# Moving one pooling product behind the first selected queries, and raising the priority of the compression inputs

## Chip, cores and metric

One NeuronCore of a Trainium2 chip. The metric is the device time of one execution in microseconds (us).

## The reference

One decoder layer on x of 512 tokens by 1024 channels. One input projection of x feeds three token mixers: A, a pooling mixer (trailing windows of 2, 4, 8 and 16 tokens, one for each of four channel groups); B, attention over the top 128 keys that an indexer picks for each query; C, attention over compressed blocks, selected blocks and a window, with gates. Each output is multiplied by a SiLU gate, projected, merged by sigmoid gates, projected again, added to x and normalised. The two parts that the change touches:

```
# A, for channel group g with window w
mean   = (running sum over the last w tokens) / min(position, w)
pooled = mean - x_g
y_g    = (pooled @ pool_w[g] + pool_b[g]) * scale_g          # then * silu(a_z)

# C, compressed keys and values: 31 blocks of 32 tokens, stride 16
blk = tok[block] + pos            # per group: 31 x (32 * 64)
h   = silu(blk @ w1)
out = h @ w2                      # kcmp from c_kc, vcmp from c_vc
```

## The kernel before, in words

Float32 products are made of three matmuls (`mm3`, lines 68 to 70): both operands are split into a high and a low part (`split`, lines 64 and 65: ScalarE writes the high part, VectorE subtracts for the low one). A dense tile (`dense`) is 128 output channels by 512 tokens, eight such triples over the 1024 input channels; its weight tile is loaded and split by `load_w` (lines 92 to 95: a DMA issued by POOL, ScalarE's copy, POOL's subtraction), two to three tiles ahead.

The order of TensorE's instructions is the order in which the program emits them. VectorE, ScalarE, POOL and SyncE are ordered by a scheduler that simulates the program on its own model and takes, among the instructions that are ready, the one with the highest priority; earlier in the program is higher, and `tc.high_priority()` raises what stands inside it. Buffers carry a tag, and tiles of one tag share a fixed number of buffers ("s" 2, "b" 6, "t" 16, dense PSUM 3, score PSUM 4): a tile can be written only when an earlier one is free.

Attention runs through a list of units. For each sub-unit `front` emits score matmuls (`qkc`, line 441), whose mask is VectorE's (443), exponent ScalarE's (448), and whose probabilities are split by both (460 and 462); `back` two sub-units later emits the products with the values (479). Between them a stream F of other work is advanced by a count of steps (`F.step`), one step for each yield. F's items are written out by hand: compression, gates, pooling, queries, merges. A string such as "c0" in the list is a marker: F stops there until the flag is set, which happens when the last unit of group 0 of mixer C is finished.

What the change touches in F:
- `compress_in(i, nm)`, for keys and then for values: loads `w1` into `w1s` (tag s) and splits it into `w1h` and `w1l`; runs a dense tile; adds bias and position in four VectorE instructions into `bk` (tag s, line 331); splits `bk` into `bkh` and `bkl`. `compress_mid` multiplies them later (names `cpk`, `cpv`).
- `pool_x(g)`: a dense tile, ScalarE's copy `x0`, g + 1 doubling sums on POOL (lines 566 and 567), VectorE's mean minus x (570 to 573), a split into `ph`. `pool_z(g)`: the gate `za`. `pool_y(g)`: one triple `ph` times the pooling weights, then VectorE (588) and a split into `YA`, which the `merge` items read.
- `f_zc(1, 1)`: the second gate tile of group 1 of mixer C. `f_qb(0, e)`: the queries of mixer B, the first work behind "c0".

In profile lines, `d` is a dense tile's PSUM, `pool` the PSUM of `pool_y`, `is` and `rel` the indexer's scores, `acc` of lines 294 to 306 the indexer's sum and its top-k.

Of the kernel before, what the change touches and what calls it, by code (L numbers as in the profile page):

```python
# [12 lines left out]
OP = mybir.AluOpType  # L13
# [21 lines left out]
def trunk(ctx, tc, a, out, dbg=None):  # L35
    nc = tc.nc
# [11 lines left out]
    def big(tag, name, dt=F32, shape=(128, 2, 512)):  # L48
        return bp.tile(list(shape), dt, tag=tag, name=name, bufs=BUFS[tag])
# [4 lines left out]
    def dps(name):  # L54
        return pd.tile([128, 512], F32, tag="pd", name=name)

    def qps(name):
        return pq.tile([128, 512], F32, tag="pq", name=name)

    def f(ap):  # L60
        return ap.bitcast(F32)

    def split(h, l, src):
        nc.scalar.activation(h, src, AF.Copy)
        nc.vector.tensor_sub(l, src, f(h))  # L65
# [35 lines left out]
    ps = qps("idle")  # L101
# [40 lines left out]
    def dense(i, s0=0, ps=None):  # L142
        wh, wl = early[i][1:] if i in early else load_w(a["wt"][i], 1024, f"w{i}")
        ps = (ps or dps)(f"d{i}")
        n = S - s0
        for k in range(KT):
            w = slice(k * 128, k * 128 + 128)
            mm3(ps[:, :n], wh[:, w], wl[:, w], X(0, k, s0), X(1, k, s0), k == 0, k == KT - 1)
            yield
        return ps[:, :n], bias[:, i:i + 1]  # L150
# [7 lines left out]
    LOW, UPP = slice(0, 64), slice(64, 128)  # L158
# [160 lines left out]
    def compress_in(i, nm):  # L319
        pos = small["pos" + nm]  # L320
        w1s = big("s", "w1s", F32, (128, 16, 64))
        w1h = big("t", "w1h", F32R, (128, 16, 64))
        w1l = big("t", "w1l", F32R, (128, 16, 64))
        nc.sync.dma_start(w1s, a["w1" + nm])
        split(w1h, w1l, w1s)
        ps, b = yield from dense(i)
        bk = big("s", "bk", F32, (128, 2, 31, 16))
        for g in range(2):
            r = (LOW, UPP)[g]
            for hf in range(2):  # L330
                nc.vector.scalar_tensor_tensor(
                    bk[64 * hf:64 * hf + 64, g],
                    ps[r, 16 * hf:16 * hf + 496].rearrange("p (n l) -> p n l", l=16), b[r],
                    pos[r, None, 16 * hf:16 * hf + 16].to_broadcast([64, 31, 16]),
                    op0=OP.add, op1=OP.add)
        bh = big("t", "bkh", F32R, (128, 62, 16))
        bl = big("t", "bkl", F32R, (128, 62, 16))
        split(bh, bl, bk.rearrange("p g n l -> p (g n) l"))
        CP[nm] = w1h, w1l, bh, bl

    def compress_w2(nm, m):
# [389 lines left out]
    for n in (2, 1, 1, 1, 1, 1, 2):  # L731
        for _ in range(n):
            st.step()
        for _ in range(n):
            st2.step()
    Stream([(index_queries, 0), (f_qc, 0, 0), (values_load,), (index_queries, 1), (f_qc, 0, 1), (values,)]).rest()
    mcmp, rowv = small["mcmp"].rearrange("p (j n) -> p j n", j=NT), small["rowv"]
    POOL[0] = True
    F = Stream([(compress_in, I_KC, "k"), (vscales,), (compress_in, I_VC, "v"), (f_zc, 0, 0), (compress_mid, "k"),
                (f_zc, 0, 1), (compress_k,), (compress_mid, "v"), (f_qc, 1, 0), (f_qc, 1, 1), (compress_v,),  # L740
                (early_g, 0, 0), (f_kk, 1), (early_g, 0, 1), (f_pool,), (f_zc, 1, 0), (pool_x, 0), (early_g, 0, 2),
                (pool_z, 0), (pool_x, 1), (early_g, 0, 3), (pool_y, 0), (pool_z, 1), (f_zc, 1, 1), (pool_x, 2), (pool_y, 1),
                (pool_z, 2), (pool_x, 3), (pool_y, 2), (pool_z, 3), (pool_y, 3),
                "c0", (f_qb, 0, 0), (f_qb, 0, 1)] + [(merge, 0, d) for d in range(3)] + [(f_zb, 0, 0), (f_zb, 0, 1)] +
               [(merge, 0, d) for d in range(3, 7)] + [(early_g, 2, 0), (merge, 0, 7)] +
               [(early_g, 2, d) for d in range(1, 4)] +
               ["c1", (f_qb, 1, 0), (f_qb, 1, 1), (f_zb, 1, 0), (f_zb, 1, 1)] + [(merge, 2, d) for d in range(KT)])
# [54 lines left out]
    for w in work:  # L802
        kind, g, j, br = w
# [91 lines left out]
    for t in range(NT):  # L895
        last = t == NT - 1
        for c0, c1 in ((512, 768), (768, 1024)) if last else ((512, 1024),):
            ps = dps("wo")
# [98 lines left out]
```

## Time and profile before

| | |
|---|---|
| median of 3 runs (lowest to highest) | 541.46 us (541.25 to 541.78) |
| profiled execution | 540.3 us, span 538.5 |
| mean granted TensorE clock | 0.982 |
| PE busy | 517.8 us (96%) |
| VectorE (DVE) busy | 377.3 us (70%) |
| ScalarE (ACT) busy | 278.1 us (52%) |
| POOL busy | 215.9 us (40%) |

The span is the time from the first to the last instruction of the profiled execution. A timeline row gives the start, the duration, the engine, the line of the kernel, the operation with its tiles (out<-in) and shape, how many instructions the row merges, and in brackets the idle time of the engine before it with what ended it. Matmuls are pipelined, so that a start follows the start before by less than the duration shown.

### The profile page before, as it was taken

Reading aid. Unit: us, or ns where it says so; the run is one execution under the profiler, and the core shown is the slowest. Engines: PE = TensorE matmul, PEld = TensorE weight load, DVE = VectorE, ACT = ScalarE, POOL = GpSimd, SP = SyncE. Lnnn points to the kernel's source line nnn. Section 1 sums busy time; section 2 is a strip of 40 time slices with the busy share of each in tenths; the row PEclk is TensorE's granted clock in tenths of the full one; section 3 lists DMA queues with packets and bytes.
Section 4 is the critical chain, followed back from the end, with each engine's and each line's share of the span. In section 5 each row is a group of like instructions: output and inputs, shape, how many; then the busy total and the mean of one; then the engine's idle time right before and its main releaser. Section 6 shows DMA issues by size and latency. Waiting matters only on the chain.

```text
span 538.5 us, 7778 instructions
## 1 busy us (share of the span) xinstructions
PE 517.8 (96%) x2718; PEld 419.3 (78%) x2718; DVE 377.3 (70%) x928; ACT 278.1 (52%) x561; POOL 215.9 (40%) x190
## 2 busy tenths in 40 slices
PE   8999999999999997799999899999999999999993
PEld 4889878888778875577788687877777888887883
DVE  5774898898769888678777887957653444544276
ACT  6783465667555767264644547666663334442000
POOL 0425433436455476126344444426662211215043
PEclk9999989999999999699999999999999999999997
DMA  7622331374464434064544645462654445453012
GB/s 275 264 79 79 103 133 60 83 152 119 147 138 119 121 90 117 23 134 130 144 120 84 146 128 107 121 130 65 181 147 121 121 139 190 158 205 126 1 65 91
DMA packets 82135, 66.72 MB, mean 124 GB/s; under 512 B 67184, under 2 KB 68656, under 8 KB 82096
## 3 DMA queue, kind: packets, MB, share of 16 engines
q1 hardware_dynamic: 74912, 40.54, 29.1%
q0 software_dynamic: 7184, 25.69, 14.9%
q8 instruction: 21, 0.34, 0.3%
q14 instruction: 18, 0.15, 0.1%
HBM read 47.87 MB, written 2.10 MB: 93 GB/s over the span
## 4 chain that ended last, share of the span: by engine, by line
PE 87%; DVE 5%; DMA 3%; ACT 2%; issue 1%; POOL 1%; SPq 0%; DVEq 0%; ACTq 0%; POOLq 0%
PE d L68 18%; PE d L69 17%; PE d L70 17%; PE acc L479 4%; PE pp L68 4%; PE qkc L441 4%; PE pp L69 4%; PE pp L70 4%; PE wo L70 3%; PE wo L69 2%; PE wo L68 2%; PE qkb L441 2%; DMA wo_st<-in_wo_dram 2%; DMA xst<-in_xT_dram 1%; PE acc L529 1%; PE ve L69 1%
## 5 line engine op out<-in xcount | busy, mean ns | idle before, releaser
L68 PE MATMUL d<-xh,w_h 128*128 128x512 f32 (+1 forms) x424 | 168.3, 397 | 0.0
L69 PE MATMUL d<-xl,w_h 128*128 128x512 f32 (+1 forms) x424 | 165.6, 391 | 0.0
L70 PE MATMUL d<-xh,w_l 128*128 128x512 f32 (+1 forms) x424 | 165.5, 390 | 0.0
L95 POOL TENSOR_TENSOR w_l<-w_st,w_h 128x1024 fp32r<-128x1024 f32 x41 | 98.1, 2394 | 128.9 <-ACT w_h L93 124.8
L68 PEld LDWEIGHTS d<-xh,w_h 128*128 128x128 f32 x424 | 80.5, 190 | 17.9 <-issue 3.2
L70 PEld LDWEIGHTS d<-xh,w_l 128*128 128x128 f32 x424 | 80.2, 189 | 17.0
L69 PEld LDWEIGHTS d<-xl,w_h 128*128 128x128 f32 x424 | 80.4, 190 | 13.8
L93 ACT ACTIVATE w_h<-w_st 128x1024 fp32r<-128x1024 f32 x53 | 56.2, 1060 | 37.0 <-DMA w_st<-in_wt_dram 26.8
L448 ACT ACTIVATE qkc<-qkc,nb 128x512 f32<-128x512 f32 (+3 forms) x64 | 32.1, 502 | 51.1 <-DVE nb L443 28.3
L95 POOL TENSOR_TENSOR wp_l<-wp_st,wp_h 128x512 fp32r<-128x512 f32 x16 | 20.6, 1288 | 52.2 <-ACT wp_h L93 52.2
L460 ACT ACTIVATE pc<-qkc,r 128x512 f16<-128x512 f32 (+3 forms) x64 | 29.6, 527 | 19.7 <-DVE r L456 8.7
L462 DVE SCALAR_TENSOR_TENSOR pc<-qkc,r,pc 128x512 f16<-128x512 f32 (+3 forms) x64 | 32.3, 545 | 9.7 <-ACT pc L460 9.2
L640 POOL TENSOR_TENSOR m<-m,tg 128x512 f32<-128x512 f32 x12 | 16.5, 1378 | 53.7 <-DVE tg L614 53.6
L443 DVE CUSTOM_DVE_ANT_0 qkc<-qkc,cmask 128x512 f32<-128x512 f32 (+3 forms) x64 | 31.3, 493 | 3.7 <-PE qkc L441 3.4
L92 POOL DMA_DIRECT2D w_st<-in_wt_dram x41 | 23.3, 569 | 10.2 <-POOL w_l L95 5.9
L70 PE MATMUL wo<-woh,ml 128*128 128x512 f32 (+1 forms) x72 | 26.4, 367 | 0.5 <-DVE ml L65 0.5
L69 PE MATMUL wo<-wol,mh 128*128 128x512 f32 (+1 forms) x72 | 26.3, 366 | 0.0
L68 PE MATMUL wo<-woh,mh 128*128 128x512 f32 (+1 forms) x72 | 26.3, 365 | 0.0
L306 DVE MATCH_REPLACE8 acc<-m,acc 128x256 f32<-128x256 f32 (+2 forms) x48 | 25.8, 541 | 0.0
L305 DVE MAX8 m<-acc 128x8 f32<-128x256 f32 (+2 forms) x48 | 25.4, 549 | 0.0
L68 PE MATMUL pp<-yh,wp_h 128*128 128x512 f32 x64 | 25.3, 395 | 0.0
L69 PE MATMUL pp<-yl,wp_h 128*128 128x512 f32 x64 | 25.0, 390 | 0.0
(249 smaller groups left out, 1003.1 us busy)
## 6 DMA issues: line engine op xcount, KB each, us to landing
w_st<-in_wt_dram POOLq DMA_DIRECT2D x41, 512.0 KB, 3.7
w_st<-in_wt_dram SPq DMA_DIRECT2D x12, 512.0 KB, 4.2
wp_st<-in_wp_dram POOLq DMA_DIRECT2D x16, 256.0 KB, 3.0
wo_st<-in_wo_dram SPq DMA_DIRECT2D x8, 512.0 KB, 3.5
xst<-in_xT_dram SPq DMA_DIRECT2D x8, 256.0 KB, 5.1
wp_st<-in_wp_dram SPq DMA_DIRECT2D x8, 256.0 KB, 2.7
z<-in_x_dram SPq DMA_DIRECT2D x4, 512.0 KB, 5.5
wvst<-in_wve_dram SPq DMA_DIRECT2D x4, 320.0 KB, 7.1
```

The lines of the kernel that those rows point to most:

```text
L68: nc.tensor.matmul(ps, wh, rh, start=start, stop=False)
L69: nc.tensor.matmul(ps, wh, rl, start=False, stop=False)
L70: nc.tensor.matmul(ps, wl, rh, start=False, stop=stop)
L93: nc.scalar.activation(h[:, :n], st, AF.Copy)
L95: eng.tensor_sub(l[:, :n], st, f(h[:, :n]))
L305: nc.vector.max(m8, negm[j])
L306: nc.vector.match_replace(negm[j], m8, negm[j], MARK)
L441: nc.tensor.matmul(ps[:, o:o + m], q, K[:, z, w], start=z == 0, stop=z == 1)
L443: nc.vector.tensor_tensor_reduce(sc[i], sc[i], self.mask, -0.125, 3e38, OP.add, OP.min, nb[:, i:i + 1])
L448: nc.scalar.activation(sc[i], sc[i], AF.Exp, scale=-1.0, bias=nb[:, i:i + 1], accum_out=den[:, i:i + 1])
L460: nc.scalar.activation(p[:, 0, i], sc[i], AF.Copy, scale=r[:, i:i + 1])
L462: self.last = nc.vector.scalar_tensor_tensor(p[:, 1, i], sc[i], r[:, i:i + 1], p[:, 0, i], op0=OP.mult, op1=OP.subtract)
```

## The change

Two edits. In `compress_in` the four VectorE additions and the split of `bk` come inside `tc.high_priority()`; the tiles `bkh` and `bkl` are declared ahead of it. In the list of F, `f_zc(1, 1)` goes from ahead of `pool_x(2)` to behind `pool_x(3)`, `pool_y(2)` from ahead of `pool_z(3)` to behind it, and `pool_y(3)` from ahead of the marker "c0" to between `f_qb(0, 0)` and `f_qb(0, 1)`.

```diff
         ps, b = yield from dense(i)
         bk = big("s", "bk", F32, (128, 2, 31, 16))
-        for g in range(2):
-            r = (LOW, UPP)[g]
-            for hf in range(2):
-                nc.vector.scalar_tensor_tensor(
-                    bk[64 * hf:64 * hf + 64, g],
-                    ps[r, 16 * hf:16 * hf + 496].rearrange("p (n l) -> p n l", l=16), b[r],
-                    pos[r, None, 16 * hf:16 * hf + 16].to_broadcast([64, 31, 16]),
-                    op0=OP.add, op1=OP.add)
         bh = big("t", "bkh", F32R, (128, 62, 16))
         bl = big("t", "bkl", F32R, (128, 62, 16))
-        split(bh, bl, bk.rearrange("p g n l -> p (g n) l"))
+        with tc.high_priority():
+            for g in range(2):
+                r = (LOW, UPP)[g]
+                for hf in range(2):
+                    nc.vector.scalar_tensor_tensor(
+                        bk[64 * hf:64 * hf + 64, g],
+                        ps[r, 16 * hf:16 * hf + 496].rearrange("p (n l) -> p n l", l=16), b[r],
+                        pos[r, None, 16 * hf:16 * hf + 16].to_broadcast([64, 31, 16]),
+                        op0=OP.add, op1=OP.add)
+            split(bh, bl, bk.rearrange("p g n l -> p (g n) l"))
         CP[nm] = w1h, w1l, bh, bl
...
-                (pool_z, 0), (pool_x, 1), (early_g, 0, 3), (pool_y, 0), (pool_z, 1), (f_zc, 1, 1), (pool_x, 2), (pool_y, 1),
-                (pool_z, 2), (pool_x, 3), (pool_y, 2), (pool_z, 3), (pool_y, 3),
-                "c0", (f_qb, 0, 0), (f_qb, 0, 1)] + [(merge, 0, d) for d in range(3)] + [(f_zb, 0, 0), (f_zb, 0, 1)] +
+                (pool_z, 0), (pool_x, 1), (early_g, 0, 3), (pool_y, 0), (pool_z, 1), (pool_x, 2), (pool_y, 1),
+                (pool_z, 2), (pool_x, 3), (f_zc, 1, 1), (pool_z, 3), (pool_y, 2),
+                "c0", (f_qb, 0, 0), (pool_y, 3), (f_qb, 0, 1)] + [(merge, 0, d) for d in range(3)] + [(f_zb, 0, 0), (f_zb, 0, 1)] +
```

## Rows read from the trace of the kernel before

**Rows 1.** The page: busy time, share of the span, instructions.

```profile
PE 517.8 (96%) x2718; PEld 419.3 (78%) x2718; DVE 377.3 (70%) x928; ACT 278.1 (52%) x561; POOL 215.9 (40%) x190
```

**Rows 2.** PE's waits: who for whom, total us, times, longest.

```profile
PE pool L68 <- ACT ph L64: 6.9, 2, 6.5
...
PE cpk L69 <- DVE bkl L65: 1.2, 1, 1.2
```

**Rows 3.** Timeline of PE around the last two pooling products.

```profile
202.79 0.40 PE L70 MATMUL d<-xh,w_l 128*128 128x512 f32 x1
203.57 0.49 PE L68 MATMUL pool<-ph,plhl 128*128 128x512 f32 x1 [0.39 <-ACT ph L64]
204.30 0.50 PE L69 MATMUL pool<-ph,plhl 128*128 128x512 f32 x1 [0.23 <-DVE ph L65]
...
212.22 0.40 PE L70 MATMUL d<-xh,w_l 128*128 128x512 f32 x1
219.11 0.80 PE L68 MATMUL pool<-ph,plhl 128*128 128x512 f32 x1 [6.50 <-ACT ph L64]
```

**Rows 4.** Stretches: length, busy PE, PEld, DVE, ACT, POOL, clock, DMA share, GB/s.

```profile
190.00:230.00 40.00, 32.88 (x162) 24.99 (x161) 31.71 (x88) 20.69 (x46) 21.07 (x24) 0.87 0.34 86
...
219.11:225.53 6.42, 6.42 (x15) 4.75 (x15) 3.72 (x8) 2.13 (x5) 0.00 (x0) 0.50 0.00 0
230.00:290.00 60.00, 60.00 (x343) 47.70 (x342) 47.75 (x136) 31.98 (x69) 26.93 (x22) 1.00 0.56 128
```

**Rows 5.** Timeline of ScalarE: copy and split of the last pooling input.

```profile
205.92 0.68 ACT L153 ACTIVATE x<-d,bias 128x512 f32<-128x512 f32 x1
...
218.43 0.63 ACT L64 ACTIVATE ph<-x 128x512 fp32r<-128x512 f32 x1 [3.21 <-DVE x L573]
```

**Rows 6.** Timeline: first matmuls of steps 9, 25 and 51; a pooling input.

```profile
195.32 0.39 PE L68 MATMUL d<-xh,w_h 128*128 128x512 f32 x1
...
228.74 0.39 PE L68 MATMUL d<-xh,w_h 128*128 128x512 f32 x1
...
179.63 0.43 PE L68 MATMUL d<-xh,w_h 128*128 128x512 f32 x1
...
172.18 0.67 DVE L65 TENSOR_TENSOR ph<-x,ph 128x512 fp32r<-128x512 f32 x1
```

**Rows 7.** Timeline: the inputs of the compression product of the keys.

```profile
72.76 0.25 PE L69 MATMUL cpk<-bkl,w1h 128*64 128x62 f32 x1 [1.21 <-DVE bkl L65]
...
68.54 1.06 ACT L64 ACTIVATE w1h<-w1s 128x1024 fp32r<-128x1024 f32 x1 [2.36 <-DMA w1s<-in_w1k_dram]
...
69.88 1.02 ACT L64 ACTIVATE bkh<-bk 128x992 fp32r<-128x992 f32 x1
...
63.61 1.68 DVE L247 SCALAR_TENSOR_TENSOR vl<-v,vscale,vh 128x640 f16<-128x640 f32 x2 [0.37 <-ACT vh L246]
...
65.61 2.97 DVE L331 SCALAR_TENSOR_TENSOR bk<-d,bias,small 64x496 f32<-64x496 f32 x4
...
69.64 1.23 DVE L65 TENSOR_TENSOR w1l<-w1s,w1h 128x1024 fp32r<-128x1024 f32 x1 [0.21 <-ACT w1h L64]
...
71.51 1.19 DVE L65 TENSOR_TENSOR bkl<-bk,bkh 128x992 fp32r<-128x992 f32 x1
...
64.52 0.33 SPq L324 DMA_DIRECT2D w1s<-in_w1k_dram  x1
```

**Rows 8.** Stretches behind two short waits, columns as in rows 4.

```profile
76.00:80.00 4.00, 4.00 (x18) 3.40 (x18) 3.97 (x7) 3.57 (x7) 0.33 (x1) 0.66 0.38 131
...
300.60:302.20 1.60, 0.13 (x2) 0.06 (x1) 1.60 (x6) 1.49 (x4) 0.60 (x1) 1.00 0.30 123
```

**Rows 9.** Timeline: a VectorE sum beside a POOL subtraction, and the next one.

```profile
60.18 2.46 DVE L296 SCALAR_TENSOR_TENSOR acc<-rel,iw,acc 128x256 f32<-128x256 f32 x1
...
62.75 0.48 DVE L296 SCALAR_TENSOR_TENSOR acc<-rel,iw,acc 128x256 f32<-128x256 f32 x1
...
59.97 2.39 POOL L95 TENSOR_TENSOR w_l<-w_st,w_h 128x1024 fp32r<-128x1024 f32 x1 [3.90 <-ACT w_h L93]
```

## The prediction

> **What bounds the kernel now.** I read the page first: TensorE (PE) is busy 517.8 of 538.5 us [rows 1]. So a change pays only where PE stands still or runs at half clock. Second, the waits of PE: two groups belong to lines that the change moves. The pooling product waited twice for its split input, 6.9 us in total, and the compression product waited once for `bkl`, 1.2 us [rows 2]. Third, PE's instructions around the pooling products: the last matmul before `pool_y(3)` starts at 212.22, the product itself only at 219.11, and `pool_y(2)` is held up twice by small waits [rows 3]. Fourth, the stretches: after the long wait PE runs 6.42 us at clock 0.50 (1.2 of 2.4 GHz), and from 230 on at 1.00 [rows 4]. These three places are the whole object of the change.
>
> **Counting the stream.** One step of the stream F is one yield: a dense tile has 8, `pool_y` has 1. Attention work is laid between steps by their count alone, so step n stands at the same place of PE's order before and after. From the point where the lists part, before: `f_zc(1,1)` 1 to 8, `pool_x(2)` 9 to 16, `pool_y(1)` 17, `pool_z(2)` 18 to 25, `pool_x(3)` 26 to 33, `pool_y(2)` 34, `pool_z(3)` 35 to 42, `pool_y(3)` 43, marker, `f_qb(0,0)` 44 to 51. After: `pool_x(2)` 1 to 8, `pool_y(1)` 9, `pool_z(2)` 10 to 17, `pool_x(3)` 18 to 25, `f_zc(1,1)` 26 to 33, `pool_z(3)` 34 to 41, `pool_y(2)` 42, marker, `f_qb(0,0)` 43 to 50, `pool_y(3)` 51. The marker's flag is set before step 42 in either list (step 42 is the dense matmul group just behind the first `kw` scores of group 1, which come after the flag), so the stream isn't held there.
>
> **Part 1, the pooling products.** Nothing is added or removed; every dense tile moves with its weight DMA and split on POOL, in the same order as its matmuls, so the queue on POOL sees the same sequence of sizes.
> - `pool_y(3)`: its input starts when `pool_x(3)` ends. That was 202.79 + 0.23 = 203.02, and the product started at 219.11: a chain of 16.1 us, ScalarE's copy at 205.92, sums on POOL, ScalarE's split at 218.43 [rows 3, 5]. Now `pool_x(3)` ends with step 25, which starts at 195.32 and takes three matmuls of 0.23: 196.0 [rows 6]. The same chain ends at 212.1. The product stands at step 51, which began at 228.74 and, with what is saved before it, would begin near 217.8 [rows 6]. So 5.7 us to spare. Saved: from 212.22 + 0.23 to 219.11 = 6.66 us.
> - The half clock behind it: 6.42 us at 0.50 [rows 4] is work of 3.21 us at full level. Saved: 3.21. It goes only if no other long wait takes its place.
> - `pool_y(2)`: 203.57 - 203.02 = 0.55 before its first matmul, and 204.30 - 203.57 - 0.23 = 0.50 before its second [rows 3]. Its input is now 34 steps old instead of 18. Saved: 1.05.
> - `pool_y(1)`: moved 8 steps nearer to its input. It would start where step 9 stood, 179.63; the second half of its input was started at 172.18 [rows 6]. Six us to spare: nothing. `f_zc(1,1)` moves 25 steps back, to about 203; the first output of group 1 that reads it is finished two score units after the first `kw` scores, later than 220: nothing.
> Sum of part 1: 6.66 + 3.21 + 1.05 = 10.92 us.
>
> **Part 2, the priority.** PE comes to the compression product at about 71.4 and stands until 72.76, when `bkl` is there [rows 7]. Before it ScalarE made `w1h` (68.54) and `bkh` (69.88), with a `rel` between; VectorE made `w1l` (69.64) and `bkl` (71.51), with score sums between [rows 7]. Without these between, `bkh` follows `w1h` at 69.6 and is there at 70.65; `bkl` follows `w1l` at 70.87 and ends at 72.06. That is 0.70 us earlier; with `bkh` first the sum is the same, because both subtractions (1.23 and 1.19) still run one behind the other. What is pushed back is score sums, and their top-k is due much later. Saved: 0.70, the value I take, because it is made of the rows of the very instructions.
> The ends lie apart. Below: the half clock after this wait (0.66 over 76 to 80, so 4.00 x 0.34 = 1.36 us lost) may go too; a wait of 1.5 us at 300.6 left the clock at 1.00 [rows 8], so a wait alone doesn't decide it. That would make 2.06. Above: `w1s` and `bk` use the same two buffers (tag s), which the value tiles free one after the other: `w1s` was issued at 64.52, just after the first `vl` (two in 1.68 us from 63.61), and `bk` ran after the second [rows 7]. If the priority lets `bk` take the first buffer, `w1s` waits for the second `vl`, now behind `bk`: 64.5 + 2.97 + 0.84 = 68.3; its data take 68.54 - 64.52 = 4.02, then 1.1 for `w1h` and 1.2 for `w1l`: 74.6, which is 1.9 later than 72.76. If the `bk` of the values takes the second buffer too, 3.4.
> VectorE's scalar_tensor_tensor `acc`, with POOL's subtraction beside it, took 2.46 us and ended 0.28 us after it; the next of the same shape took 0.48 [rows 9]. The Trainium skill, SBUF — State Buffer, Who interferes with whom, says that a VectorE instruction with two SBUF inputs and a GpSimd instruction that reads SBUF shut each other out, whichever starts first; the trace agrees. By that rule `bkl`, moved ahead, could come to stand behind a POOL subtraction. One such collision costs what the row shows, 2.46 - 0.48 = 1.98, and turns -0.70 into +1.28.
>
> **Sum.** 10.92 + 0.70 = 11.62 us. The profiled execution took 540.3 (span 538.5 and 1.8 around it); the median of the runs is 541.46, 1.16 above. 540.3 - 11.62 = 528.7 for that execution, **529.8** for the median.
>
> **The rivals.**
> - *VectorE becomes the bound.* In 190 to 230 it is busy 31.71 of 40 us [rows 4]; without 10.92 PE needs 29.1. VectorE then lacks 2.6 us, at most: 532.4. Against: in 230 to 290 it has 12 us free (47.75 of 60) [rows 4], score tiles have four PSUM banks, and products are used two units later. The collision on the port, at 531.8, counts here.
> - *The priority backfires*, as worked out above: 529.8 + 0.7 + 1.9 = 532.4, or 533.9 with 3.4, up to 535 if the half clock lasts longer. For: both tiles really wait for a buffer at 64.5. Against: `w1s` only needs SyncE, which is idle, while VectorE has the second `vl` ready.
> - *The stall moves.* The new plan of VectorE, ScalarE and POOL puts `pool_x(3)`'s chain more than 5.7 us later. Each further us costs one, and a long wait brings the half clock back: 534 to 540.
> - *The other side: the input of `pool_y(3)` waits for a buffer.* Its copy, its two live sums, `za` of group 2, and the `z` of `f_zc(1,1)` and of `pool_z(3)` share six buffers (tag b). If the copy can only start when `pool_y(2)`, now at step 42, frees one (about 210.7 for the product, 2.8 for what follows it: 213.5), then with the 2.9 us that ScalarE took before it, 202.79 + 0.23 to 205.92, and 13.2 from there to the product [rows 3, 5], it ends at 229.6: 11.8 after 217.8, and 3.2 of half clock. 15.0 - 11.6 = 3.4 slower, 544.9. It decides from a product later than 226.2. Against: I count five live buffers at the time of the copy.
> - *It doesn't do what it says:* the scheduler keeps the order of part 2, or a new wait of equal size elsewhere eats part 1 (541).
>
> **How the numbers follow.** Forecast (529.8, within 1): 0.40. With the half clock of part 2 gone too (528.4): 0.12. Priority backfires (532 to 535): 0.22. VectorE or the port (531 to 532.4): 0.08. Stall moves (534 to 540): 0.06. No effect (541): 0.05. Slower (544.9 or a like case): 0.07. A measurement of this kernel tells about 0.2%, 1.1 us, from no change. Faster: 0.40 + 0.12 + 0.22 + 0.08 + 0.06 = 0.88; same 0.05; slower 0.07. The range takes in the first four cases, 0.82: 527.5 to 535.5.
>
> **What would show it.** Right: no wait of a pooling product over 0.5 us, no half clock between 200 and 230, `bkl` ending near 72.1. Wrong: a PE wait at `f_qb(0,0)` or at `pool_y(3)`; `w1s` issued after 68 and PE waiting for `w1l`; score matmuls waiting for VectorE between 200 and 230.

## The result, and the profile after

The changed kernel takes 537.63 us (median of 6 runs, 535.33 to 538.98); the kernel before took 541.07 (538.97 to 541.78) beside it. The ratio is 0.9936, interval [0.9909, 0.9963]: about 3.4 us faster. The direction was right; the time was 7.8 us above the forecast and outside the range. The profiled execution took 538.19 us (span 536.4).

The page of the changed kernel, busy time and share of the span:

```profile
PE 517.9 (97%) x2718; PEld 419.2 (78%) x2718; DVE 378.9 (71%) x928; ACT 277.7 (52%) x561; POOL 217.8 (41%) x190
```

PE's waits in the changed kernel (total us, times, longest), to be set against [rows 2]:

```profile
PE pool L68 <- ACT ph L64: 3.7, 1, 3.7
PE pp L68 <- ACT tg L603: 1.5, 1, 1.5
...
PE wo L70 <- DVE ml L65: 1.1, 1, 1.1
PE cpk L69 <- DVE bkl L65: 1.0, 1, 1.0
```

Of the waits of pooling products one is left: `pool_y(2)` doesn't wait any more, `pool_y(3)` still does, 3.7 us instead of 6.5. The same in PE's timeline (`pool_y(2)`, then the end of the first selected queries, then `pool_y(3)`), which answers to [rows 3]:

```profile
210.69 0.40 PE L68 MATMUL pool<-ph,plhl 128*128 128x512 f32 x1
...
217.06 0.39 PE L70 MATMUL d<-xh,w_l 128*128 128x512 f32 x1
221.62 0.62 PE L68 MATMUL pool<-ph,plhl 128*128 128x512 f32 x1 [3.72 <-ACT ph L64]
```

And in stretches (length, busy PE, PEld, DVE, ACT, POOL, clock, DMA share, GB/s), to be set against [rows 4] and [rows 8]:

```profile
76.00:80.00 4.00, 3.75 (x32) 3.26 (x31) 3.94 (x7) 3.20 (x6) 1.34 (x2) 1.00 0.42 142
190.00:230.00 40.00, 36.17 (x191) 28.19 (x191) 36.24 (x99) 24.13 (x52) 19.70 (x20) 0.96 0.40 102
221.62:225.61 3.99, 3.88 (x9) 2.80 (x10) 3.99 (x9) 3.95 (x7) 1.48 (x2) 0.57 0.00 0
...
285.00:310.00 25.00, 23.53 (x130) 18.14 (x128) 18.36 (x72) 14.48 (x44) 9.59 (x8) 0.93 0.47 119
```

In 190 to 230 PE is busy 36.17 us where it was 32.88, VectorE 36.24 where it was 31.71. Behind the wait PE still runs 3.99 us at clock 0.57, near the lower level (1.2 of 2.4 GHz), 1.7 us lost. At 285 to 310 the clock is 0.93; in the kernel before it was 1.00 in the same stretch, behind a wait of the same 1.5 us.

Now the chain that `pool_y(3)` waits for: ScalarE's copy of the tile, POOL's doubling sums (the first, third and fourth are shown), VectorE's steps and ScalarE's split. From the timelines of the three engines in the changed kernel:

```profile
199.22 0.70 ACT L153 ACTIVATE x<-d,bias 128x512 f32<-128x512 f32 x1
...
201.79 1.03 POOL L567 TENSOR_TENSOR xs<-x 128x511 f32<-128x511 f32 x1
...
204.81 1.05 POOL L567 TENSOR_TENSOR xs<-xs 128x508 f32<-128x508 f32 x1
205.81 0.32 POOL L568 COPY xs<-xs 128x4 f32<-128x4 f32 x1
208.26 2.38 POOL L95 TENSOR_TENSOR w_l<-w_st,w_h 128x1024 fp32r<-128x1024 f32 x1 [2.13 <-ACT w_h L93]
210.59 1.73 POOL L567 TENSOR_TENSOR xs<-xs 128x504 f32<-128x504 f32 x1
212.27 0.19 POOL L568 COPY xs<-xs 128x8 f32<-128x8 f32 x1
...
214.47 0.88 DVE L305 MAX8 m<-acc 128x8 f32<-128x384 f32 x2
215.27 0.36 DVE L571 TENSOR_TENSOR pe<-xs,small 128x15 f32<-128x15 f32 x1
...
218.82 0.75 DVE L573 SCALAR_TENSOR_TENSOR x<-xs,x 128x512 f32<-128x512 f32 x1
...
220.10 0.16 DVE L574 COPY x<-pe 128x15 f32<-128x15 f32 x1
...
220.95 0.62 ACT L64 ACTIVATE ph<-x 128x512 fp32r<-128x512 f32 x1
```

The copy is 6.7 us earlier than before, the split 2.5 us later: from copy to split 21.7 us, where [rows 5] gave 12.5. Two places make the difference. POOL had the third sum's small copy done at 206.13, then stood 2.13 us for ScalarE's half of a weight split, subtracted for 2.38 us, and only then began the fourth sum. That weight belongs to `f_qb(0, 1)`, the tile behind the product, whose first matmul starts at 223.36, 12.7 us after the subtraction ended; `load_w` stands under high priority, the sums don't. In the kernel before, what stood between the third and the fourth sum was the half-size weight of a merge. From the timelines of POOL and VectorE in the kernel before:

```profile
213.12 1.27 POOL L95 TENSOR_TENSOR wp_l<-wp_st,wp_h 128x512 fp32r<-128x512 f32 x1 [0.47 <-ACT wp_h L93]
214.35 1.25 POOL L566 TENSOR_TENSOR xs<-xs 128x504 f32<-128x504 f32 x1
215.53 0.66 POOL L567 COPY xs<-xs 128x8 f32<-128x8 f32 x1
...
216.23 0.17 DVE L570 TENSOR_TENSOR pe<-xs,small 128x15 f32<-128x15 f32 x1
...
218.22 0.17 DVE L573 COPY x<-pe 128x15 f32<-128x15 f32 x1
```

From the third sum's end to the fourth's: 6.3 us after, 3.5 before. And from there to the split: 212.46 to 220.95, 8.5 us, where the kernel before took 216.19 to 218.43, 2.2. In the kernel before VectorE began 0.04 us after the sum was there and made its four steps one behind the other. In the changed kernel the sum lay ready for 2.8 us: VectorE stood 0.7 us for ScalarE's part of some probabilities, which came ahead in its order, then did them and two top-k maxima, and came to its first step at 215.27. Between that step and the last, at 220.10, stand 11 instructions of other work (masks, top-k rounds, gates), with no break. So in the end the split did not wait for the late sum but for the place of these steps in VectorE's order.

### The profile page after: what moved, and what is told of

It is laid out like the page before. It is cut to its first block, busy times and chain, and to the rows that moved or that the text cites. A ratio compares the mean times of both kernels' runs of the same rounds, so it can differ in the third digit from the quotient of the medians.

```text
span 536.4 us, 7778 instructions
## 1 busy us (share of the span) xinstructions
PE 517.9 (97%) x2718; PEld 419.2 (78%) x2718; DVE 378.9 (71%) x928; ACT 277.7 (52%) x561; POOL 217.8 (41%) x190
## 4 chain that ended last, share of the span: by engine, by line
PE 44%; DMA 6%; DVE 5%; ACT 3%; issue 1%; DVEq 0%; ACTq 0%
PE d L68 7%; PE d L70 7%; PE d L69 7%; PE pp L68 3%; PE pp L69 3%; PE acc L480 3%; PE pp L70 3%; DMA wo_st<-in_wo_dram 3%; DMA w_st<-in_wt_dram 3%; PE wo L70 3%; PE wo L69 2%; PE wo L68 2%; PE qkb L442 2%; PE qkc L442 1%; DVE wol L65 1%; DVE w_l L95 1%
## 5 line engine op out<-in xcount | busy, mean ns | idle before, releaser
L461 ACT ACTIVATE pc<-qkc,r 128x512 f16<-128x512 f32 (+3 forms) x64 | 29.5, 526 | 17.4 <-DVE r L457 8.5
L95 DVE TENSOR_TENSOR w_l<-w_st,w_h 128x1024 fp32r<-128x1024 f32 x12 | 15.6, 1306 | 14.6 <-ACT w_h L93 14.6
```

Of the source, the lines that this page charges most:

```text
L95: eng.tensor_sub(l[:, :n], st, f(h[:, :n]))
L461: nc.scalar.activation(p[:, 0, i], sc[i], AF.Copy, scale=r[:, i:i + 1])
```

## The experiments

Copy and split of the last pooling input, and the wait of its product, in all kernels but the priority alone, where they are as before (read from the timelines; single executions differ by up to 3.7 us from their beginning on, so the length is what compares). "Between" counts VectorE's instructions of other work between its first and its last step on this input:

| kernel | copy | fourth sum | split | copy to split | between | wait of the product | ratio to before |
|---|---|---|---|---|---|---|---|
| before | 205.92 | 214.35 | 218.43 | 12.5 | 0 | 6.50 | 1 |
| changed | 199.22 | 210.59 | 220.95 | 21.7 | 11 | 3.72 | 0.9936 |
| product later still | 199.09 | 210.46 | 220.81 | 21.7 | 11 | none | 0.9923 |
| changed, top-k postponed | 201.76 | 211.64 | 219.14 | 17.4 | 6 | none | 0.9811 |
| last product alone | 204.61 | 213.04 | 217.93 | 13.3 | 2 | 0.98, 1.93 | 0.9886 |
| old list, top-k postponed | 205.30 | 213.14 | 217.22 | 11.9 | 0 | 6.75 | 0.9946 |
| last product, top-k postponed | 205.48 | 213.34 | 217.99 | 12.5 | 2 | 1.00, 0.70 | 0.9834 |
| changed, more top-k | 199.62 | 210.24 | 221.52 | 21.9 | 14 | 4.58 | 0.9914 |
| changed, fourth sum first | 198.97 | 205.96 | 213.05 | 14.1 | 2 | none | 0.9841 |
| changed, fourth sum on VectorE | 201.53 | 212.25 | 215.76 | 14.2 | 2 | none | 0.9904 |
| fourth sum first, top-k postponed | 197.47 | 204.35 | 211.81 | 14.3 | 2 | none | 0.9775 |

Wherever the chain takes 17 us or more, six or more instructions of other work stand between VectorE's steps; wherever it takes under 15, two at most. How busy VectorE is in 190 to 230 doesn't set this alone: 11 stand between at 36.24 us of 40, two at 37.41.

**The priority alone.** The kernel before with the second edit and its old list.

```diff
+        with tc.high_priority():
+            ... the four additions and the split of bk
```

> The kernel before with the priority of the compression inputs alone; the list is as before. Theory A (the priority changes nothing: VectorE and ScalarE have bk, bkh and bkl at the same places of their order in the kernel after as in the kernel before): the same time as before, ratio 1.000 within 0.3%, PE's wait at the compression product 1.0 to 1.3 us with bkl between two score sums. Rival B (the priority is worth the 0.7 to 2.1 us of the prediction): 0.996 to 0.999 and the wait near 0.5.

541.77 us, ratio 0.9996 [0.9971, 1.002]. PE's waits:

```profile
PE pool L68 <- ACT ph L64: 6.9, 2, 6.5
PE pp L68 <- ACT tg L603: 1.5, 1, 1.5
PE cpk L69 <- DVE bkl L65: 1.3, 1, 1.3
```

Nothing moved: VectorE, ScalarE, POOL and SyncE have their instructions in the same order in this trace as in that of the kernel before, and the first three in the changed kernel too, up to 150 us, where the lists don't differ yet. Part 2 of the sum was worth nothing; the interval alone would leave room for its 0.70 us, the unmoved order and the wait of 1.3 us do not. Why the priority passed nothing wasn't tested; my reading is that the scheduler starts each of these instructions as soon as its own model has the inputs ready.

**The product later still.** The changed kernel, `pool_y(3)` behind both tiles of the selected queries.

```diff
-                "c0", (f_qb, 0, 0), (pool_y, 3), (f_qb, 0, 1)] + ...
+                "c0", (f_qb, 0, 0), (f_qb, 0, 1), (pool_y, 3)] + ...
```

> The kernel after with the last pooling product behind f_qb(0,1) instead of behind f_qb(0,0), 8 steps later. Theory A (the product waits 3.9 us because its input's chain is late by that much, and nothing else is late): the wait and the half clock behind it go, 5.9 us less than the kernel after, near 531.7, ratio to before 0.983; PE waits at most 1 us where the first merge reads the product. Rival B (VectorE is over-full between 190 and 230, so that PE stands somewhere in any case): a wait of 2 us or more moves to a score product, a dense tile or the merge, and the time stays within 1.5 us of 537.6.

537.85 us, ratio 0.9923 [0.99, 0.9946]: the same as the changed kernel. PE's timeline, the product and the first merges behind it:

```profile
224.35 0.50 PE L68 MATMUL pool<-ph,plhl 128*128 128x512 f32 x1
...
232.28 0.50 PE L68 MATMUL pp<-yah,wp_h 128*128 128x512 f32 x1 [2.40 <-ACT yah L64]
...
235.00 0.79 PE L69 MATMUL pp<-yal,wp_h 128*128 128x512 f32 x1 [2.22 <-DVE yal L65]
```

The product itself doesn't wait now, but the merge that reads its result does, 4.6 us in two waits. The split of the input stood at 220.81, as late as in the changed kernel. That is the outcome that rival B gave, and theory A's 531.7 fell; that VectorE's fullness is the reason, this run doesn't show. A place further back doesn't help: the input has to come earlier.

**The top-k postponed**, run twice: 529.24 us, ratio 0.9775 [0.9738, 0.9812], and on another chip 530.43, 0.9811 [0.9785, 0.9838]. No top-k rounds in sub-units 11 to 15, more of them behind, the same count in all.

```diff
-                tk(1.7)
+                tk(0 if 11 <= nsub < 16 else 2.5 if 16 <= nsub < 27 else 1.7)
```

> The kernel after with the top-k rounds of five sub-units (between about 180 and 220 us) postponed and made up for later: some 8 rounds of about 1.1 us of VectorE work less in that stretch, the same work in all. Theory A (the chain's VectorE steps stand behind other work in VectorE's queue): the input of the last product is there 3 us earlier or more, its wait falls from 3.7 to under 1 us, the half clock goes; 4 to 6 us less than after if the postponed rounds are hidden. Rival B (POOL, with the weight subtraction that stands ahead of the fourth sum, makes it late): the fourth sum ends at the same time, the wait falls by less than 1 us, the time is as after.

> The third run's kernel once more (the changed kernel with the top-k rounds postponed), on the chip and in the rounds of the three above, so that they can be compared with it directly. Theory VectorE's load: 528 to 531, no wait of a pooling product over 1 us. Rival (the third run's gain was in part a matter of that chip's runs): 533 or more.

The second of the two, split and product in the timelines of ScalarE and PE, and the stretch:

```profile
219.14 0.62 ACT L64 ACTIVATE ph<-x 128x512 fp32r<-128x512 f32 x1
...
219.81 0.50 PE L68 MATMUL pool<-ph,plhl 128*128 128x512 f32 x1
```

```profile
190.00:230.00 40.00, 39.02 (x218) 30.08 (x217) 33.40 (x80) 27.23 (x61) 20.53 (x23) 1.00 0.41 104
```

The wait and the half clock behind it are gone and VectorE is busy 2.8 us less. At this point I took VectorE's load for the cause. But the chain is still 17.4 us long, the split is only 1.8 us earlier, and PE came to the product 2 us later than in the changed kernel; the input was ready just in time. Of the 6.8 us by which this execution is shorter than the changed kernel's, 4.0 are gained from 205 to 226, around the product, 2.1 behind the merge's wait at 285 to 310, where no half clock followed this time, and 1.5 at the end; 0.9 were lost before (read from the starts of the same matmuls in both traces). The postponement also changed VectorE's order: 6 instructions of other work stand between the steps on this input instead of 11. The gain is shown, load as its cause is not.

**The last product alone**, the kernel before with `pool_y(3)` moved and `f_zc(1, 1)`, `pool_y(2)` left in place.

```diff
-                (pool_z, 2), (pool_x, 3), (pool_y, 2), (pool_z, 3), (pool_y, 3),
-                "c0", (f_qb, 0, 0), (f_qb, 0, 1)] + ...
+                (pool_z, 2), (pool_x, 3), (pool_y, 2), (pool_z, 3),
+                "c0", (f_qb, 0, 0), (pool_y, 3), (f_qb, 0, 1)] + ...
```

> The kernel before with one edit: the last pooling product goes from ahead of the marker to behind f_qb(0,0); its input tile pool_x(3) and the other items stay. Theory A (moving the input tile up 8 steps bought nothing, since the chain took 25.5 us instead of 16.1): the chain ends near 219 as before, the product is due near 218.8, so a wait under 1.5 us and no half clock; the two small waits of pool_y(2) stay; 8 to 10 us less than before, ratio 0.982 to 0.986. Rival B (the place of the input tile is what helps): the product waits 3 us or more, ratio 0.992 or above.

535.12 us, ratio 0.9886 [0.9849, 0.9923]. PE's timeline:

```profile
218.61 0.50 PE L68 MATMUL pool<-ph,plhl 128*128 128x512 f32 x1 [0.98 <-ACT ph L64]
221.04 0.50 PE L69 MATMUL pool<-ph,plhl 128*128 128x512 f32 x1 [1.93 <-DVE ph L65]
```

With the input's copy 5.4 us later than in the changed kernel, its split came 3.0 us earlier (217.93 against 220.95), and the medians favour it by 2.5 us, though the intervals overlap. The outcome lies between the two expectations: 2.9 us of waits where theory A had at most 1.5, and 6.3 us gained instead of 8 to 10; rival B's ratio of 0.992 or more did not come. Moving the input tile up made its split later, not earlier.

**Old list, and the last product alone, both with the top-k postponed.** The edits above, combined.

> The kernel before with its own list and without the priority; only the top-k rounds of VectorE are moved, none during sub-units 11 to 15 and 2.5 in place of 1.7 in each of sub-units 16 to 26 (the same count in all). Theory A (the stall of the kernel before is made of the distance between the last pooling input and its product; VectorE's queue adds only the 2.2 us between POOL's last sum and ScalarE's split): the product still waits 4.5 to 6.5 us, half clock follows, and the time is 537 to 541. Theory B (VectorE's load alone makes every stall of this place, so taking it away is enough whatever the list): the wait falls under 2 us, VectorE is under 30 us busy in 190 to 230, and the time is 528 to 532, the same as the new list with the postponement.

> The kernel before with the last pooling product alone moved (between the two tiles of the first selected queries), the input tile left where it was, no priority, and the top-k rounds postponed as in the third run. Theory A (once VectorE is relieved the chain from the last pooling input to its product takes about 16 us, and the product at step 51 stands far enough behind it): waits of pooling products under 2 us in total, and 528.5 to 531, so that moving the input tile up buys nothing even then. Theory B (the nearer distance of 26 steps to the product's step is still too short; the input tile has to move up as well): the product waits 2.5 us or more, some half clock follows, and the time is 532 to 535, at least 2.5 above the changed kernel with the postponement.

The old list: 538.58 us, 0.9946 [0.9919, 0.9974]. The last product alone: 531.29, 0.9834 [0.9809, 0.9859]. The products in PE's timeline, the old list first, with its stretch:

```profile
217.91 0.80 PE L68 MATMUL pool<-ph,plhl 128*128 128x512 f32 x1 [6.75 <-ACT ph L64]
```

```profile
190.00:230.00 40.00, 33.25 (x169) 25.87 (x168) 26.84 (x62) 21.69 (x48) 22.48 (x26) 0.91 0.38 90
```

```profile
218.67 0.50 PE L68 MATMUL pool<-ph,plhl 128*128 128x512 f32 x1 [1.00 <-ACT ph L64]
219.87 0.69 PE L69 MATMUL pool<-ph,plhl 128*128 128x512 f32 x1 [0.70 <-DVE ph L65]
```

With the old list the wait stays at 6.75 us although VectorE is busy only 26.84 of 40 us in 190 to 230: theory A there, the stall of the kernel before was the distance from input to product and not VectorE. With the product moved the same relief leaves 1.7 us of waits, under the 2 of theory A, in a time 0.3 us above its bound; with the input tile moved up as well the median is 0.9 us lower (530.43 on the same chip), which the intervals don't tell apart.

**More top-k in the stretch.** The changed kernel, the dose the other way.

```diff
-                tk(1.7)
+                tk(2.5 if 11 <= nsub < 16 else 1.3 if 16 <= nsub < 26 else 1.7)
```

> The changed kernel with more of VectorE's top-k in the stretch of the pooling products: 2.5 rounds in place of 1.7 in sub-units 11 to 15, and 1.3 in place of 1.7 in sub-units 16 to 25, the same count in all; some 4 rounds, about 3.5 to 4 us of VectorE work, come into a stretch where it was busy 36.24 of 40 us. Theory A (VectorE's load sets when the last pooling input is split, and so the wait): the split of the input ends later by about the work added, the product's wait grows from 3.88 us to 6 or more, and the time to 540 to 544. Theory B (the chain is late because of POOL's sums and the collision with a subtraction, not because of the load): the wait stays between 3 and 5 us and the time at 536.5 to 539.

535.96 us, ratio 0.9914 [0.9884, 0.9945], not told apart from the changed kernel. PE's timeline:

```profile
222.19 0.80 PE L68 MATMUL pool<-ph,plhl 128*128 128x512 f32 x1 [4.58 <-ACT ph L64]
```

Four more top-k rounds (30 instructions of line 306 between 180 and 235, where the changed kernel has 22), 4.0 us of VectorE's work with their maxima, made the chain 0.2 us longer, and the wait 0.9. Theory A's size is missed by far. So load alone was not the cause, and the order of POOL's queue came under suspicion.

**The fourth sum first.** The changed kernel; the weight subtraction of `f_qb(0, 1)` is queued behind the fourth sum of `pool_x(3)` on POOL.

```diff
-            eng.tensor_sub(l[:, :n], st, f(h[:, :n]))
+            PL["n"] = PL.get("n", 0) + ("last" in PL)
+            with tc.issue_after(PL["last"].ins) if PL["n"] == 4 else ExitStack():
+                eng.tensor_sub(l[:, :n], st, f(h[:, :n]))
...
-            nc.gpsimd.tensor_copy(nxt[:, :sft], cur[:, :sft])
+            cpy = nc.gpsimd.tensor_copy(nxt[:, :sft], cur[:, :sft])
+            if i == 3:
+                PL["last"] = cpy
```

> The changed kernel with one swap in POOL's queue: the weight subtraction for the tile of the first selected queries stands behind the fourth doubling sum of the last pooling input instead of ahead of it (in the changed kernel POOL had the third sum done at 206.1, stood 2.1 us for that tile's split weights and did the subtraction, and began the fourth sum at 210.59). TensorE's and SyncE's orders are unchanged; the scheduler then puts the input's last VectorE step 12 places further ahead. Theory P (the late input is made in the order of POOL's queue, and VectorE's load only adds to it): the fourth sum starts near 206 to 207, ScalarE's split near 214 to 217, ahead of the product's place at 217.7; no wait of the product over 0.7 us, and 531 to 533.5. Theory V (VectorE's load of over 90% alone decides when the input is ready): the split stays behind 219, the product waits 2 us or more, and the time stays at 535.5 to 538.

531.48 us, ratio 0.9841 [0.9808, 0.9873]. POOL, VectorE, ScalarE and PE in the timelines, and the stretch:

```profile
205.96 1.27 POOL L569 TENSOR_TENSOR xs<-xs 128x504 f32<-128x504 f32 x1
207.16 0.19 POOL L570 COPY xs<-xs 128x8 f32<-128x8 f32 x1
208.01 2.39 POOL L97 TENSOR_TENSOR w_l<-w_st,w_h 128x1024 fp32r<-128x1024 f32 x1 [0.65 <-ACT w_h L93]
...
211.01 0.15 DVE L575 TENSOR_TENSOR pe<-xs,small 128x15 f32<-128x15 f32 x1
...
212.76 0.17 DVE L578 COPY x<-pe 128x15 f32<-128x15 f32 x1
...
213.05 0.63 ACT L64 ACTIVATE ph<-x 128x512 fp32r<-128x512 f32 x1
...
217.44 0.39 PE L68 MATMUL pool<-ph,plhl 128*128 128x512 f32 x1
```

```profile
190.00:230.00 40.00, 40.00 (x227) 31.80 (x226) 35.88 (x100) 24.96 (x54) 19.34 (x20) 1.00 0.41 103
```

This is the state that the prediction described. The sum takes the idle time in which POOL had stood for the weight, so the subtraction isn't delayed: it begins 9.04 us after the tile's copy, as in the changed kernel (208.26 - 199.22). The chain falls from 21.7 to 14.1 us: 4.9 up to the fourth sum, and 2.8 behind it. PE is busy for all of the 40 us, at full clock. And VectorE is as full as in the changed kernel, 35.88 us against 36.24: theory V falls. Behind the stretch a merge waits 1.8 us for the queries' low part, a wait that the changed kernel doesn't have.

The one edge changed two orders, though: POOL's, and VectorE's, where the scheduler now puts the steps on this input further ahead (the last by 12 places), with two instructions of other work between them. In the changed kernel VectorE came to the sum 2.8 us after it was there, because other work stood ahead in its order. With VectorE's order left as it was, an earlier sum would only have lain ready longer. So by the traces the gain comes through VectorE's new order, and the swap on POOL is what brought the scheduler to it; no run has the one without the other.

**The fourth sum on VectorE.** The changed kernel, that sum and its copy off POOL.

```diff
-            nc.gpsimd.tensor_add(nxt[:, sft:], cur[:, sft:], cur[:, :S - sft])
-            nc.gpsimd.tensor_copy(nxt[:, :sft], cur[:, :sft])
+            eng = nc.vector if i == 3 else nc.gpsimd
+            eng.tensor_add(nxt[:, sft:], cur[:, sft:], cur[:, :S - sft])
+            eng.tensor_copy(nxt[:, :sft], cur[:, :sft])
```

> The changed kernel with the fourth doubling sum of the last pooling input and its small copy made by VectorE instead of POOL, some 0.9 us more work on VectorE and the same result. Theory P: the sum no longer stands behind the weight subtraction, so the input is split at 217 to 219 and the product waits 1.5 us at most; 532.5 to 535. Theory V: one more instruction on the full engine makes the input later or leaves it at 221; the wait is 3.5 us or more, and the time is 537 to 539.

535.68 us, ratio 0.9904 [0.9869, 0.9938]. VectorE, ScalarE and PE in the timelines, and the stretch:

```profile
212.25 1.23 DVE L568 TENSOR_TENSOR xs<-xs 128x504 f32<-128x504 f32 x1
...
215.76 0.63 ACT L64 ACTIVATE ph<-x 128x512 fp32r<-128x512 f32 x1
...
220.03 0.39 PE L68 MATMUL pool<-ph,plhl 128*128 128x512 f32 x1
```

```profile
190.00:230.00 40.00, 38.79 (x223) 30.43 (x221) 37.41 (x102) 25.52 (x57) 19.46 (x22) 1.00 0.40 103
```

More work on the fuller engine (37.41 of 40 us), and the chain is 7.5 us shorter; the product doesn't wait. Theory V falls again. But the wait behind POOL's subtraction is not what was saved: the fourth sum stood 3.8 us in VectorE's queue and was done only 1.2 us sooner behind the copy (12.0 us instead of 13.2). The other 6.3 us lie behind the sum, where VectorE's steps follow almost at once. That is the order of VectorE again. The time is 0.7 above theory P's bound; other waits came up: 1.2 us for VectorE's `za`, 0.8 for the queries' low part, 1.9 for ScalarE ahead of a dense tile at 289.

**Both.** The fourth sum first and the top-k postponed.

> The changed kernel with both: the top-k rounds postponed as in the third run, and the swap in POOL's queue. There the third run's product found its input 0.05 us after PE was ready, with ScalarE's split at 219.2. Theory P: the split comes at 213 to 216, several us before the product's place; the time is that of the third run or up to 1 us less, 528 to 530.5, because no wait is left there. Theory V: the split stays near 219 and the time at 529 to 531; then the swap does nothing that the postponement has not done.

528.52 us, ratio 0.9775 [0.9743, 0.9807], together with the first run of the postponement the fastest kernel of the study. ScalarE and PE in the timelines:

```profile
211.81 0.65 ACT L64 ACTIVATE ph<-x 128x512 fp32r<-128x512 f32 x1
...
214.33 0.39 PE L68 MATMUL pool<-ph,plhl 128*128 128x512 f32 x1
```

The chain is about as long as with the swap alone (14.3 us): once the order is right, the load has no say in it. What the postponement adds to the swap is not settled. In the two profiled executions 2.9 of 4.1 us lie at the compression product at 70 to 84, where the swap alone ran at half clock and this one did not, and neither edit touches that place.

## Why the prediction was wrong, step by step

- *The stream's steps.* Right: `pool_x(3)` ended at 196.1 (196.0 worked out), PE was ready for `pool_y(3)` at 217.9 (217.8).
- *`pool_y(2)` and `pool_y(1)`.* Right: no wait of either, 1.05 us saved.
- *`pool_y(3)`.* This is the step that failed: "The same chain ends at 212.1." ScalarE's copy came 3.1 us behind the tile, as before (2.9), but the split of the input started at 220.95: the chain from copy to split was no constant, it took 21.7 us instead of 12.5. The ground for it was a sentence ahead of the list, "so the queue on POOL sees the same sequence of sizes". That is true of the weights alone. The sums of `pool_x(3)` kept their time behind the tile, while the weights came at other steps, so another and larger subtraction fell between the third and the fourth sum, of a weight that was not needed for another 12.7 us. That is 2.8 of the 9.2 us by which the chain grew. The other 6.3 are VectorE's: its steps on the sum stood behind and between other work, 8.5 us from sum to split instead of 2.2, and the prediction didn't look at VectorE's order at all. The swap, which changed both orders, gave 14.1 us from copy to split, still 1.6 more than in the kernel before, and no wait, as forecast.
- *The half clock behind it.* Wrong for the same reason: 1.7 us of it stayed.
- *The priority, 0.70.* Wrong: nothing moved. The wait for `bkl` was 0.96 us instead of 1.21, with the same order of instructions.
- *VectorE becomes the bound.* As worked out, a matter of busy time, it did not decide: with 35.88 of 40 us busy PE had no wait. But the order of VectorE's queue was the larger part of the longer chain (6.3 of 9.2 us). *The stall moves* was the case that came, with the time it gave (534 to 540), and had a chance of 0.06; its mechanism, a new plan of the three engines, was named, but no row was looked for that would show it coming. One was there: POOL's subtraction between two sums of this very chain. The new place of VectorE's steps could not be read from the trace of the kernel before, where they followed the sum at once.
- *The buffer wait* did not come: the copy started 3.1 us after the tile.
- *The sum.* The profiled execution is 9.5 us above the 528.7 worked out for it. By the starts of the same matmuls in both traces: 5.6 us are the wait of `pool_y(3)` and the half clock behind it, 1.5 the half clock behind the merge's wait at 297, 0.7 a wait for a weight's low part at 455, 0.9 around the last projection's wait (1.1 us, 0.5 before), and 0.8 the priority and the beginning.

The Trainium skill's rule of "SBUF — State Buffer", Who interferes with whom, had nothing to decide at `bkl`, since that was not moved.

## What to carry to other kernels

A chain that passes through the queues of shared engines is not a constant that can be moved with its first instruction: list what stands between its steps on each engine's queue, and ask what stands there in the new order. When an input tile is moved up and its product still waits, look for the steps whose data lie ready before their engine takes them up, whether it stands idle for another input (POOL, 2.1 us) or has other work ahead in its order (VectorE, 2.8 us); one edge on one engine was worth more here than the whole move, and it moved another engine's order with it. An engine that is 90% busy is a suspect and not yet a cause: with the load unchanged and the order different, the wait was gone.

## What was not expected of the hardware

Short waits of PE are followed by half clock in one execution and not in another. The plainest pair is the kernel before and the priority alone, whose instructions stand in the same order: at 76 to 80 the clock was 0.66 and 1.00, at 285 to 310 it was 1.00 and 0.93, behind waits that differ by 0.1 us at most. Behind the wait for `bkl` (1.0 to 1.3 us) the stretch 76 to 80 had clock 1.00 in the changed kernel, 0.52 with the fourth sum first, and 1.00 with both edits. Behind the merge's wait of 1.5 us the stretch 285 to 310 had 0.93 in the changed kernel and 1.00 with the fourth sum first. By the starts of the same matmuls in two traces such a half clock cost 1.5 us behind the merge's wait (changed kernel against before) and 2.9 behind the wait for `bkl` (fourth sum first against both edits), as much as many an edit. What decides it is left open.
